# Splitting the output projection of the differential attention over heads, with part of it done amid the attention

## The chip, the cores and the metric

The kernel runs on one core of a Trainium2 chip. Its time is the device time of one execution in microseconds (us); the median of several executions is compared. The engines are TensorE (PE in the profile, its weight loads as PEld), VectorE (DVE), ScalarE (ACT), GpSimd (POOL) and SyncE (SP), which only issues transfers here. Each engine runs its instructions in the order in which they were laid out when the program was built.

## What is computed

One inference step of a decoder of two layers: layer 0 mixes tokens by gated linear attention, layer 1 by differential attention, and each is followed by an MLP with squared ReLU. There is a prompt of 1024 tokens (16 meta tokens ahead of it) and eight running sequences with one new token each, which read a paged cache. The part that matters here is the prompt in layer 1:

```python
def diff_core(q, k, v, q_pos, k_pos, lam):
    s = jnp.einsum('bqhmd,bkhmd->bhmqk', q, k).astype(F32) * (DIFF_DH ** -0.5)
    ...
    p = jax.nn.softmax(s, axis=-1)
    a = p[:, :, 0] - lam * p[:, :, 1]
    return jnp.einsum('bhqk,bkhe->bqhe', a, v.astype(F32))

def diff_output(o, g_sub, lam_init, w_out, dtype):
    B, T = o.shape[:2]
    o = rms_norm(o, g_sub) * (1.0 - lam_init)
    return o.reshape(B, T, DIFF_HEADS * DIFF_DV).astype(dtype) @ w_out

def post_norm(x, f, g, b):
    return layer_norm(DEEPNORM_ALPHA * x + f, g, b)
```

There are 8 heads; each has two score maps (m = 0, 1) of 64 dimensions and values of 128. The outputs of the heads stand side by side in 1024 columns, so the 1024 rows of w_out belong to the heads, 128 rows each, and the product with w_out is a sum over heads. It is added to the residual and normalised.

## The kernel before

Everything is in fp32 accuracy. Where a product has to keep it, each operand is split into a high part (rounded to fp32r) and the remainder, and three matmuls are made for one: high*high, high*low, low*high (`mm3`, L185 to L188). Weights come in pieces of 128x512 by DMA into `raw` (2 buffers); ACT rounds a piece into `whi` (L173) and POOL subtracts to give `wlo` (L174). A unit of 256 columns is a `whi`/`wlo` pair of 2048 columns, of which there are two.

A tile framework allocates buffers from rotating pools and puts each engine's instructions in order when the program is built, by a timeline of its own. So an instruction can stand before or behind where the source has it. PSUM has three pools: `mmt` (3 buffers), `axt` (3) and `smt` (2).

Attention of layer 1 (L1225 to L1251) goes over heads 0 to 7 and in each over eight blocks of 128 queries, called tiles, in the order 7, 1, 5, 3, 6, 0, 4, 2 (head 7: 3, 2, 1, 0, 7, 6, 5, 4); tile t sees 16 + 128(t + 1) keys. With the first tile of a head, `prep` makes the keys and queries of the next: loads on SP, transposes on TensorE (L1134, L1139, L1144), the split by ACT and VectorE (L182, L183), and nine moves by DMA from POOL's queue (L1150 to L1156). A tile (`tile_`, L1159 to L1202) then does:

- scores on TensorE into `mmt` (L1178, L1179; head 0: L1174 to L1176), in up to three pieces for each of the two maps;
- mask and running minimum on VectorE (L1182) into a score buffer `as` of pool `scp` (5 buffers, 8.3 KB in each partition);
- exponent with row sum on ACT (L1184), and the combination of the two maps on VectorE (L1186 to L1188);
- transposes on TensorE into `axt` (L1197), a copy on ACT into `aT` (L1199, pool `a3`, 6 buffers), and the product with the values on TensorE into `smt` (L1202).

After each four tiles the result goes to `Y` (L1237) with its sum of squares (L1238, L1239). `o_norm` (L1206 to L1214) scales pairs of heads: after heads 1, 3 and 5 two heads at a time, after head 6 that one, with the power and the multiply on POOL; head 7's two halves are multiplied on VectorE. `o_fm` (L1216 to L1222) transposes one head's output of 512 tokens (`c` = 0 or 1) into `XH` and `XL` (high and low), by four transposes (L1220), one ACT copy and one VectorE operation. All eight heads' `o_fm` for c = 0 stand behind tile 3 of head 7, all for c = 1 behind the last tile. `Y` serves for the outputs of the heads until then; afterwards the residual, which was put aside in DRAM (`xres`), is loaded back into the same memory (L1261, eight DMAs).

Then `w_out` (L882 to L908) multiplies: four units of 256 columns (u) by two halves of the tokens (c), in the order written at L886, with two PSUM tiles of 48 matmuls each (2 blocks of tokens, 8 heads, 3 matmuls), 768 in all, and adds each tile to the residual in `Y` (L900). Weights of a unit are loaded when first named. After its fifth tile stands the w_out of the eight running sequences (`samples`, L1300 to L1313). `normalize` (L918) takes the finished rows, `to_fm` (L944) transposes them for the MLP, whose weights and buffers (`hp`, `HF`, `rwp`) get their memory when the attention's pools close.

Of the kernel before, what the change touches and what calls it, by code (L numbers as in the profile page):

```python
# [11 lines left out]
F32 = mybir.dt.float32  # L12
F32R = mybir.dt.float32r
# [3 lines left out]
ALU = mybir.AluOpType  # L17
# [12 lines left out]
FF = 4096  # L30
NPG = 32
ALPHA = 4.0 ** 0.25
EPS = 1e-5
# [77 lines left out]
def hybrid_step(ctx, tc, A, dbg=None, upto=9):  # L111
# [769 lines left out]

    def w_out(w, scaled, side=None):  # L882

        units = {}
        n = 0
        for u, c in ((0, 0), (1, 0), (0, 1), (1, 1), (2, 0), (3, 0), (2, 1), (3, 1)):  # L886
# [3 lines left out]
            for i2 in range(2):  # L890
                ps = mmt()
                t0 = 4 * c + 2 * i2
                for i in range(2):
                    a = slice((t0 + i) * P, (t0 + i + 1) * P)
                    for k in range(NB):
                        mm3(ps[:, i * 256 : (i + 1) * 256], XH[:, k, a], XL[:, k, a], hv[:, k, :], lv[:, k, :], k == 0, k == NB - 1)
                yv = Yt[:, t0 : t0 + 2, u * 256 : (u + 1) * 256]
                pv = ps.rearrange("p (i n) -> p i n", n=256)
                if scaled:
                    V.tensor_tensor(yv, yv, pv, op=ALU.add)  # L900
                else:
                    steps_v.append(V.scalar_tensor_tensor(yv, yv, ALPHA, pv, ALU.mult, ALU.add).ins)
                if side and (n == 4 if scaled else n < 5):
# [127 lines left out]
    paged = decode()  # L1031
    normalize(w_out(A["gla_w_out"][0], False, paged), stats, lambda c: to_fm(c, 0))
    normalize(mlp(paged), stats, lambda c: to_fm(c, 1))
# [181 lines left out]

    def o_fm(h, c):  # L1216
        cs = slice(512 * c, 512 * c + 512)
        ps = axt()
        for i in range(4):
            TE.transpose(ps[:, i * P : (i + 1) * P], Yt[:, 4 * c + i, h * P : (h + 1) * P], ident)  # L1220
        S.activation(XH[:, h, cs], ps, AF.Copy, scale=gs)
        V.scalar_tensor_tensor(XL[:, h, cs], ps, gs, XH[:, h, cs].bitcast(F32), ALU.mult, ALU.subtract)  # L1222
# [29 lines left out]

# [5 lines left out]
    rwp = e.enter_context(tc.tile_pool(name="rwp", bufs=5))  # L1258
    for c in range(2):
        for u in range(4):  # L1260
            dma(Yt[:, 4 * c : 4 * c + 4, u * 256 : (u + 1) * 256], A["xres"][512 * c : 512 * c + 512, u * 256 : (u + 1) * 256].rearrange("(t p) n -> p t n", p=P))  # L1261
    CH = TH // 2

    HF = hp.tile([P, NB, 2, TH], F32, name="HF")

# [306 lines left out]
```

## Time and profile before

| | |
|---|---|
| runs | 2924.56, 2924.34, 2919.79 us; median 2924.34 us |
| span of the profiled execution, first to last instruction | 2919.7 us |
| busy share of the span | PE 95%, DVE 65%, ACT 36%, POOL 39% |
| mean granted TensorE clock | 0.976 |
| attention of layer 1 | about 1814 to 2089 us of the span |
| its w_out, with the normalisation and the transposes amid it | about 2089 to 2194 us |
| DMA over the whole span | 636 MB, 218 GB/s |

The profiled execution's own time isn't listed apart from its span; the span is 0.1 us under the lowest run. In the views, a group of instructions stands as line, engine, operation, output<-inputs, shape and count, then busy us in total, mean ns of one, and the idle time before them with what ended it. In a window's row come busy us (and count) of PE, PEld, DVE, ACT and POOL, then the granted clock (1.00 is full), the busy share of the DMA engines and GB/s. A wait reads "engine, tile and line <- what it waited for: us in total, times, longest". The ends of matmuls are modelled, so a busy TensorE needn't be at its peak rate.

### The profile page before, as it was taken

The numbers are of one execution on the slowest core, as the hardware profiler recorded it, in microseconds if no ns is written. First come the engines' busy times: TensorE is split into PE (matmuls) and PEld (weight loads), VectorE is DVE, ScalarE is ACT, GpSimd is POOL, SyncE is SP. The second block draws the span as 40 slices with busy tenths as digits, with TensorE's granted clock in tenths as the row PEclk, the third lists the DMA queues.
The fourth block names the chain that finished last, engine by engine and source line by source line (L and its number), as shares of the span: only waits on it lengthen the run. The fifth ranks groups of instructions, "written<-read, shape, count | busy, mean of one in ns | idle before, by whom it ended". The sixth has DMA issues, their size and how long they took to land. (4 is left out here: it accounts for less than half of the span.)

```text
span 2919.7 us, 52085 instructions
## 1 busy us (share of the span) xinstructions
PE 2779.7 (95%) x19653; PEld 2277.6 (78%) x19653; DVE 1891.2 (65%) x2982; ACT 1044.1 (36%) x2075; POOL 1133.7 (39%) x867
## 2 busy tenths in 40 slices
PE   8889999999999999999999998889998999999997
PEld 5666767987777777777898896778888889797885
DVE  2564644457877777777667942788638855838478
ACT  3233453251222122122321112667524535335352
POOL 2230222233333334334233331132335766677664
PEclk9899999999999999999999998999999999999998
DMA  7557651514798988988387999363436778595893
GB/s 257 178 185 251 233 177 37 198 56 141 242 350 297 335 309 298 346 317 321 137 275 252 348 343 314 75 139 86 119 112 205 195 207 232 152 281 129 257 246 87
DMA packets 285366, 636.46 MB, mean 218 GB/s; under 512 B 25510, under 2 KB 141292, under 8 KB 273852
## 3 DMA queue, kind: packets, MB, share of 16 engines
q1 hardware_dynamic: 252716, 520.66, 51.6%
q0 software_dynamic: 32400, 112.50, 15.9%
q8 instruction: 154, 2.52, 0.4%
q14 instruction: 96, 0.79, 0.1%
HBM read 575.55 MB, written 44.06 MB: 212 GB/s over the span
## 5 line engine op out<-in xcount | busy, mean ns | idle before, releaser
L174 POOL TENSOR_TENSOR wlo<-raw,whi 128x512 fp32r<-128x512 f32 x256 | 360.0, 1419 | 744.0 <-ACT whi L173 670.8
L186 PE MATMUL mmt<-whi,XH 128*128 128x256 f32 (+1 forms) x1760 | 527.4, 302 | 2.9 <-ACT Y L310 2.0
L187 PE MATMUL mmt<-wlo,XH 128*128 128x256 f32 (+1 forms) x1760 | 527.8, 301 | 0.7 <-POOL wlo L174 0.7
L186 PE MATMUL mmt<-XH,whi 128*128 128x512 f32 (+1 forms) x1216 | 438.1, 361 | 7.4 <-DVE HL L183 7.2
L188 PE MATMUL mmt<-whi,XL 128*128 128x256 f32 x1536 | 437.2, 286 | 0.1
L188 PE MATMUL mmt<-XH,wlo 128*128 128x512 f32 (+1 forms) x1216 | 434.4, 358 | 0.0
L790 DVE TENSOR_REDUCE sc<-pg 128x16 f32<-128x1024 f32 x256 | 309.7, 1214 | 93.4 <-POOL pg L789 90.1
L173 ACT CAST whi<-raw 128x512 fp32r<-128x512 f32 x256 | 152.9, 619 | 578.4 <-PE mmt L188 191.1
L186 PEld LDWEIGHTS mmt<-whi,XH 128*128 128x128 f32 x1760 | 333.4, 190 | 30.1 <-issue 15.6
L187 PEld LDWEIGHTS mmt<-wlo,XH 128*128 128x128 f32 x1760 | 334.8, 190 | 28.2 <-issue 16.8
L187 PE MATMUL mmt<-XL,whi 128*128 128x512 f32 x768 | 307.3, 400 | 0.0
L188 PEld LDWEIGHTS mmt<-whi,XL 128*128 128x128 f32 x1536 | 292.1, 191 | 9.9 <-issue 8.8
L789 DVE TENSOR_TENSOR pg<-pg,qb 128x1024 f32<-128x1024 f32 x192 | 256.8, 1343 | 62.1 <-DMA pg<-in_cache_k 38.1
L186 PEld LDWEIGHTS mmt<-XH,whi 128*128 128x128 f32 x1216 | 231.7, 191 | 55.1 <-issue 13.7
L789 POOL TENSOR_TENSOR pg<-pg,qb 128x1024 f32<-128x1024 f32 x64 | 158.6, 2478 | 293.5 <-DMA pg<-in_cache_k 236.7
L188 PEld LDWEIGHTS mmt<-XH,wlo 128*128 128x128 f32 x1216 | 231.8, 191 | 35.8 <-issue 3.8
L186 PE MATMUL mmt<-whi,HH 128*128 128x512 f32 x512 | 205.6, 402 | 1.7 <-DVE Y L1014 1.7
L187 PE MATMUL mmt<-wlo,HH 128*128 128x512 f32 x512 | 204.7, 400 | 0.0
L188 PE MATMUL mmt<-whi,HL 128*128 128x512 f32 x512 | 203.9, 398 | 0.0
L187 PEld LDWEIGHTS mmt<-XL,whi 128*128 128x128 f32 x768 | 145.4, 189 | 39.6 <-issue 8.8
L1416 POOL TENSOR_TENSOR wlo<-RW,whi 128x512 fp32r<-128x512 f32 x96 | 156.3, 1749 | 37.1 <-ACT whi L1415 37.0
L1416 POOL TENSOR_TENSOR wlo<-rw,whi 128x512 fp32r<-128x512 f32 x92 | 147.7, 1674 | 41.4 <-ACT whi L1415 41.2
(441 smaller groups left out, 5769.3 us busy)
## 6 DMA issues: line engine op xcount, KB each, us to landing
pg<-in_cache_k SPq DMA_DIRECT2D x256, 512.0 KB, 6.0
pg<-in_cache_v SPq DMA_DIRECT2D x256, 512.0 KB, 6.0
XH<-xc POOLq DMA_DIRECT2D x42, 1032.0 KB, 7.9
raw<-in_mlp_w SPq DMA_DIRECT2D x164, 256.0 KB, 3.5
swt<-in_mlp_w SPq DMA_DIRECT2D x32, 1024.0 KB, 5.6
rw<-in_mlp_w SPq DMA_DIRECT2D x116, 256.0 KB, 3.8
RW<-in_mlp_w POOLq DMA_DIRECT2D x96, 256.0 KB, 6.0
xc<-XH POOLq DMA_DIRECT2D x14, 1032.0 KB, 6.8
```

Source lines behind the costliest of these rows:

```text
L173: S.copy(hi[:, c], raw)
L174: G.tensor_tensor(lo[:, c], raw, hi[:, c].bitcast(F32), op=ALU.subtract)
L186: TE.matmul(ps, ah, bh, start=first, stop=False)
L187: TE.matmul(ps, ah, bl, start=False, stop=False)
L188: TE.matmul(ps, al, bh, start=False, stop=last)
L789: eng.tensor_tensor(pg, pg, qb, op=ALU.mult)
L790: return V.tensor_reduce(sc[:, n, :], pg.rearrange("p (h d) -> p h d", d=64), op=ALU.add, axis=AX.X).ins
L1416: G.tensor_tensor(lo[:, k, :], t, hi[:, k, :].bitcast(F32), op=ALU.subtract)
```

## The change

The rows of w_out are split between heads 0 to 2 (`EH = 3`) and heads 3 to 7.

*Early part.* A generator, `early_out`, is stepped from the loop over heads. Its first six steps (head 2, tiles 0 to 3; head 3, n = 0 and 2) run `o_fm` for heads 0 to 2 into new buffers `OH` and `OL` (12 KB each in a partition). The other sixteen steps each make one PSUM tile of 18 matmuls (2 blocks of tokens, 3 heads, 3 matmuls) for one u and one pair of token blocks: at head 3, n = 4 and 6; heads 4, 5 and 6, n = 0, 2, 4 and 6; head 7, n = 0 and 1. ACT copies the tile to an `aT` buffer, and a DMA from POOL's queue adds it to `xres` in DRAM (256 KB each). The weights of the three heads for one u (768 columns) lie in the free end of the two `XL` buffers and are loaded, rounded and subtracted anew after each four tiles (`halves_of`).

*Room.* The pool of score buffers has 4 instead of 5. `o_norm` on POOL comes after head 1 (heads 0 and 1), head 2 (that head), head 4 (heads 3 and 4) and head 6 (heads 5 and 6).

*Late part.* `o_fm` of heads 3 to 7 writes to places 0 to 4 of `XH` and `XL`. The residual is loaded back in two halves, each behind the `o_fm` of its half. `late_out` goes over the two halves of the tokens outside and the four units inside, keeps all four units' weights (two in `whi`/`wlo`, two in `WF`, which shares its memory with `HF`), and makes 16 PSUM tiles of 30 matmuls, 480 in all. `samples` follows the third of them instead of the fifth.

```diff
-    def w_out(w, scaled, side=None):
+    def w_out(w, side):
...
-    scp = e.enter_context(tc.tile_pool(name="scp", bufs=5))
+    scp = e.enter_context(tc.tile_pool(name="scp", bufs=4))
...
-    def o_fm(h, c):
+    def o_fm(h, c, hi=None, lo=None):
         cs = slice(512 * c, 512 * c + 512)
+        if hi is None:
+            hi, lo = XH[:, h - EH, cs], XL[:, h - EH, cs]
...
+    def reload(c):
+        for u in range(4):
+            dma(Yt[:, 4 * c : 4 * c + 4, u * 256 : (u + 1) * 256], A["xres"][512 * c : 512 * c + 512, u * 256 : (u + 1) * 256].rearrange("(t p) n -> p t n", p=P))
+
+    OH = a1.tile([P, EH, T], F32R, name="OH")
+    OL = a1.tile([P, EH, T], F32R, name="OL")
+    wo = A["diff_w_out"][0].rearrange("(k p) n -> p k n", p=P)
+    wv_ = [x.rearrange("p a n -> p (a n)")[:, 3088 : 3088 + 256 * EH] for x in XL.t]
+
+    def halves_of(hi, lo, k0, u):
+        for x in range(0, hi.shape[1], 512):
+            w = min(512, hi.shape[1] - x)
+            raw = wrp.tile([P, 512], F32, name="raw")
+            dma(raw[:, :w].rearrange("p (k n) -> p k n", n=256), wo[:, k0 + x // 256 : k0 + (x + w) // 256, u * 256 : (u + 1) * 256])
+            S.copy(hi[:, x : x + w], raw[:, :w])
+            G.tensor_tensor(lo[:, x : x + w], raw[:, :w], hi[:, x : x + w].bitcast(F32), op=ALU.subtract)
+
+    def out_tile(xh, xl, w, nk, t0):
+        hv, lv = (x.rearrange("p (k n) -> p k n", n=256) for x in w)
+        ps = mmt()
+        for i in range(2):
+            a = slice((t0 + i) * P, (t0 + i + 1) * P)
+            for k in range(nk):
+                mm3(ps[:, i * 256 : (i + 1) * 256], xh[:, k, a], xl[:, k, a], hv[:, k, :], lv[:, k, :], k == 0, k == nk - 1)
+        return ps
+
+    def early_out():
+        halves_of(*wv_, 0, 0)
+        for h in range(EH):
+            for c in range(2):
+                cs = slice(512 * c, 512 * c + 512)
+                o_fm(h, c, OH[:, h, cs], OL[:, h, cs])
+                yield
+        for u in range(4):
+            for t0 in range(0, 8, 2):
+                ps = out_tile(OH, OL, wv_, EH, t0)
+                o = a3.tile([P, 4, P], F32, name="aT").rearrange("p j q -> p (j q)")
+                S.copy(o, ps)
+                nc.gpsimd.dma_start(A["xres"][t0 * P : (t0 + 2) * P, u * 256 : (u + 1) * 256].rearrange("(i p) n -> p i n", p=P), o.rearrange("p (i n) -> p i n", n=256), accum_op=ALU.add)
+                if t0 == 6 and u < 3:
+                    halves_of(*wv_, 0, u + 1)
+                yield
...
             if n == 3 and h == 7:
                 o_norm(V, slice(0, 4), slice(7, 8))
-                for j in range(8):
+                for j in range(EH, 8):
                     o_fm(j, 0)
-        if h < 6 and h % 2:
-            o_norm(G, slice(0, 8), slice(h - 1, h + 1))
-        elif h == 6:
-            o_norm(G, slice(0, 8), slice(6, 7))
+                reload(0)
+            if h == 2 and n < 4 or h == 3 and n in (0, 2, 4, 6) or 3 < h < 7 and n % 2 == 0 or h == 7 and n < 2:
+                next(early)
+        if h in (1, 2, 4, 6):
+            o_norm(G, slice(0, 8), slice(2 if h == 2 else h - 1, h + 1))
     o_norm(V, slice(4, 8), slice(7, 8))
-    for j in range(8):
+    for j in range(EH, 8):
         o_fm(j, 1)
+    reload(1)
     e.close()
...
+    def late_out():
+        side, n, us = samples(), 0, []
+        for c in range(2):
+            for u in range(4):
+                if c == 0:
+                    if u < 2:
+                        w = [wsp.tile([P, 2048], F32R, name=x)[:, :LW] for x in ("whi", "wlo")]
+                    else:
+                        w = [WF[:, x : x + LW] for x in (2 * LW * (u - 2), 2 * LW * (u - 2) + LW)]
+                    halves_of(*w, EH, u)
+                    us.append(w)
+                for t0 in (4 * c, 4 * c + 2):
+                    ps = out_tile(XH, XL, us[u], NB - EH, t0)
+                    yv = Yt[:, t0 : t0 + 2, u * 256 : (u + 1) * 256]
+                    V.tensor_tensor(yv, yv, ps.rearrange("p (i n) -> p i n", n=256), op=ALU.add)
+                    if n == 2:
+                        next(side)
...
-    normalize(w_out(A["diff_w_out"][0], True, samples()), stats, lambda c: to_fm(c, 2, xr))
+    normalize(late_out(), stats, lambda c: to_fm(c, 2, xr))
+    HF = hp.tile([P, NB, 2, TH], F32, name="HF", tag="HF")
```

More of the change, by code (lines that the diff above doesn't have):

```diff
@@ L31 @@
 NPG = 32
+EH = 3
 ALPHA = 4.0 ** 0.25
@@ L1031, in hybrid_step @@
     paged = decode()
-    normalize(w_out(A["gla_w_out"][0], False, paged), stats, lambda c: to_fm(c, 0))
+    normalize(w_out(A["gla_w_out"][0], paged), stats, lambda c: to_fm(c, 0))
     normalize(mlp(paged), stats, lambda c: to_fm(c, 1))
@@ L1225, in hybrid_step @@
+    early = early_out()
     nxt = prep(0)
@@ L1258, in hybrid_step @@
     rwp = e.enter_context(tc.tile_pool(name="rwp", bufs=5))
-    for c in range(2):
-        for u in range(4):
-            dma(Yt[:, 4 * c : 4 * c + 4, u * 256 : (u + 1) * 256], A["xres"][512 * c : 512 * c + 512, u * 256 : (u + 1) * 256].rearrange("(t p) n -> p t n", p=P))
     CH = TH // 2
-    HF = hp.tile([P, NB, 2, TH], F32, name="HF")
+    LW = 256 * (NB - EH)
+    WF = hp.tile([P, NB, 2, TH], F32R, name="WF", tag="HF").rearrange("p a c n -> p (a c n)")
     RX = hp.tile([P, 4 * TH], F32, name="RX")
```

15 lines of the change are left out of this document (8 added, 7 removed).

## The prediction

> **What bounds the kernel now.** I read the page first (span, engine shares, clock), then windows over the attention and over w_out of layer 1, then the waits of the attention.
>
> ```profile
> span 2919.7 us, 52085 instructions
> PE 2779.7 (95%) x19653; PEld 2277.6 (78%) x19653; DVE 1891.2 (65%) x2982; ACT 1044.1 (36%) x2075; POOL 1133.7 (39%) x867
> PE 21%; DVE 6%; DMA 5%; issue 3%; POOL 2%; ACT 1%; DVEq 0%; POOLq 0%; ACTq 0%
> ```
>
> TensorE is busy for 95% of the span, so a matmul is only cheaper elsewhere if TensorE idles there. Windows (columns: busy us of PE, PEld, DVE, ACT, POOL with counts, then granted clock, DMA share, GB/s): heads 3 to 7 as a whole, then head by head in their first and second halves, then w_out, and a dense stretch of matmuls of 128x256.
>
> ```profile
> 1917.00:2089.00 172.00, 156.18 (x1129) 142.02 (x1128) 144.32 (x450) 121.73 (x285) 41.45 (x47) 0.96 0.43 99
> 1917.00:1930.00 13.00, 10.78 (x59) 8.18 (x58) 12.56 (x44) 9.55 (x22) 3.06 (x6) 0.93 0.57 135
> 1930.00:1951.00 21.00, 21.00 (x169) 20.82 (x168) 17.43 (x61) 15.73 (x37) 1.53 (x3) 0.96 0.63 108
> 1951.00:1963.00 12.00, 10.54 (x67) 7.98 (x66) 11.46 (x38) 10.20 (x25) 4.37 (x4) 1.00 0.57 152
> 1963.00:1984.00 21.00, 17.42 (x134) 16.77 (x133) 17.09 (x45) 12.38 (x31) 6.78 (x8) 0.92 0.49 103
> 1984.00:1997.00 13.00, 11.06 (x64) 9.13 (x63) 12.22 (x43) 9.67 (x25) 3.56 (x7) 0.87 0.43 99
> 1997.00:2016.00 19.00, 19.00 (x155) 18.71 (x154) 15.85 (x60) 15.29 (x39) 1.02 (x2) 1.00 0.40 88
> 2049.00:2089.00 40.00, 37.19 (x287) 33.90 (x288) 28.81 (x81) 25.93 (x57) 9.99 (x7) 1.00 0.25 80
> 2089.00:2194.00 105.00, 103.84 (x787) 91.17 (x786) 39.83 (x81) 25.62 (x39) 38.92 (x27) 1.00 0.46 143
> 2160.00:2181.00 21.00, 21.00 (x181) 21.00 (x180) 12.25 (x35) 7.61 (x9) 1.39 (x2) 1.00 0.08 27
> 2222.00:2240.00 18.00, 16.01 (x121) 15.79 (x121) 16.79 (x14) 12.01 (x27) 15.23 (x15) 0.91 0.75 197
> 2240.00:2257.00 17.00, 8.35 (x66) 7.93 (x65) 16.89 (x10) 3.37 (x6) 10.92 (x11) 0.86 0.82 236
> ```
>
> A head takes about 33 us and has two halves. In the first 12 or 13 us VectorE is full (12.56 of 13, 11.46 of 12, 12.22 of 13) and TensorE issues one matmul per 0.2 us; here masks and minima set the pace. In the rest TensorE is full in two of three heads (21.00 of 21, 19.00 of 19) and VectorE has 3 to 4 us to spare; here transposes and A*V set it. Over heads 3 to 7 TensorE idles 172 - 156.18 = 15.8 us. w_out behind it is TensorE alone: 103.84 of 105. The waits of eight heads (us in total, times, longest) say the same from both sides:
>
> ```profile
> DVE as L1182 <- PE mmt L1179: 23.9, 22, 4.5
> PEld mmt L1178 <- DVE ast L1182: 11.6, 25, 1.3
> PE axt L1197 <- DVE as L1188: 7.1, 5, 3.5
> ```
>
> VectorE waits for score matmuls twice as long as these wait for VectorE to free PSUM, so extra matmuls ahead of scores also hurt VectorE.
>
> **The change part by part.** One matmul of 128x256 costs, start to start, 21.00/181 = 0.116 us (the 2160 window).
>
> *Late w_out.* The rows of w_out that ran after the attention:
>
> ```profile
> L187 PE MATMUL mmt<-wlo,XH 128*128 128x256 f32 x230 | 65.2, 285 | 0.0
> L186 PE MATMUL mmt<-whi,XH 128*128 128x256 f32 x229 | 64.9, 287 | 0.5 <-ACT whi L173 0.5
> L188 PE MATMUL mmt<-whi,XL 128*128 128x256 f32 x229 | 64.7, 284 | 0.0
> L174 POOL TENSOR_TENSOR wlo<-raw,whi 128x512 fp32r<-128x512 f32 x12 | 15.3, 1281 | 38.9 <-ACT whi L173 38.9
> ```
>
> That is 688 of 768. The changed kernel has 480 (5 heads of 8), and its order puts 56 of them ahead of the last A*V, so 424 follow: 264 fewer, 264 x 0.116 = 30.6 us off the path. Against it, hand-over: the order of SyncE puts the third raw piece of unit 1 behind the reloads of the residual, which wait for the last o_fm, and units 2 and 3 convert into a region that is free only after the attention. Before, whole units were ready (idle 0.5 us). Two chunks (one load and one ACT and POOL conversion, 1.28 us each on POOL) can be late: 0 to +6 us, taken +3, as unit 0 (two tiles of 30 matmuls, 7 us) covers part.
>
> *Early blocks.* 16 blocks of 18 matmuls are added inside heads 3 to 7: 288 x 0.116 = 33.4 us of TensorE. Ends: 0, if all falls where VectorE sets the pace; +33.4, if all falls where TensorE does. The order of the changed kernel puts the blocks behind bursts of score matmuls, about half of them in either half of a head, and the idle TensorE is 15.8 us. Taking that as filled: 33.4 - 15.8 = +17.6. Each block also has one ACT copy and an accumulating DMA of 256 KB issued by POOL; their nearest rows:
>
> ```profile
> L1199 ACT COPY aT<-axt 128x512 f32<-128x512 f32 x64 | 36.8, 581 | 24.7 <-PE axt L1197 24.4
> RW<-in_mlp_w POOLq DMA_DIRECT2D x96, 256.0 KB, 6.0
> ```
>
> The copy is 0.58 us ( ACT has 50 us idle in these 172). The DMA, 6.0 us to landing, is one of 16 in 140 us at a DMA share of 0.43, and the reload that reads them comes some 30 us after the last (head 7's second tile against the end of the attention): cost nothing. If POOL is late, the copy's aT buffer (one of six) comes back late and the copies for A*V wait; that is the third rival.
>
> *Weights of heads 0 to 2.* Four sets, each of a 512 and a 256 column piece, on ACT and POOL. Three come amid heads 4 to 6. POOL works 41 of 172 us there, so its own time is free. But:
>
> ```profile
> 1899.28 4.73 DVE L1188 SCALAR_TENSOR_TENSOR as<-as,ast 128x528 f32<-128x528 f32 x1
> 1899.78 3.65 POOL L1214 TENSOR_TENSOR Y<-Y,orr 128x2048 f32<-128x2048 f32 x1
> L174 POOL TENSOR_TENSOR wlo<-raw,whi 128x512 fp32r<-128x512 f32 x8 | 10.5, 1326 | 37.9 <-ACT whi L173 37.9
> ```
>
> The combine L1188 of this width took 4.73 us and ended when POOL's multiply did. If each subtract holds up VectorE once, three sets cost 3 x (1.33 + 0.7) = 6 us; ends 0 and +6, taken +1, since VectorE is combining for under a fifth of the time and a 1.3 us overlap is a third of the one shown. The Trainium skill, "SBUF — State Buffer", section "SBUF: two separate sides", calls the port pair of VectorE and GpSimd an exclusive lock held for the whole instruction, when VectorE reads two SBUF inputs against a GpSimd operation that reads SBUF; the two rows agree (4.73 us beside 3.65). By that rule alone every subtract that meets a combine blocks it, and the sum would come out 5 us higher than mine.
>
> *Score buffers, five to four.* A fifth tile's mask must now wait until the transposes of the tile four before it have read their buffer. In head 4, tile 7's last transposes and the first mask of the fourth tile after it (464 wide):
>
> ```profile
> 1961.19 0.27 PE L1197 MATMUL axt<-c_ident,as 128*128 128x128 f32 x1
> 1959.98 0.63 DVE L1182 CUSTOM_DVE_ANT_0 as<-mmt,cmask 128x464 f32<-128x464 f32 x1
> ```
>
> The mask began 1.5 us before the transposes ended; it would now wait, in the half that VectorE bounds, and the masks and combines behind it on VectorE with it. That is the worst kind of tile (tile 7, once per head): 0 to 8 x 1.5 = 12 us; taken +3, as the queue behind it has slack in the second half.
>
> *o_fm of heads 0 to 2* moves from head 7 and after it into heads 2 and 3: six times four transposes, one ACT copy, one VectorE operation.
>
> ```profile
> L1221 ACT ACTIVATE XH<-axt,gs 128x512 fp32r<-128x512 f32 x15 | 10.1, 687 | 5.0 <-PE axt L1220 4.9
> L1222 DVE SCALAR_TENSOR_TENSOR XL<-axt,gs,XH 128x512 fp32r<-128x512 f32 x13 | 9.7, 748 | 7.0 <-ACT XH L1221 6.9
> ```
>
>  On VectorE 6 x 0.75 = 4.5 us are added where it is nearly full, and as much is taken from the end: 0 to +4, taken +1. The o_norm pieces stay four multiplies on POOL.
>
> *Start of the attention.* The mask table's buffer lies elsewhere, and its fill and load now wait for the last of decode.
>
> ```profile
> 1802.22 0.33 DVE L1102 MEMSET cmask<- 128x320 f32 x1 [11.56 <-SPq L756]
> 1813.76 0.23 DVE L846 COPY oT<-smt 128x4 f32<-128x4 f32 x2 [7.82 <-PE smt L844]
> 1814.31 0.53 DVE L1182 CUSTOM_DVE_ANT_0 as<-mmt,cmask 128x352 f32<-128x352 f32 x1 [0.32 <-DVE oT L846]
> raw<-in_mlp_w SPq DMA_DIRECT2D x164, 256.0 KB, 3.5
> ```
>
> Before, the fill was 11 us ahead of the first mask. Now it stands directly ahead: at least the 0.33, at most that and a load (3.5 us for one four times as large); taken +2.
>
> *Behind w_out.* With tokens outer, the first 512 tokens are done with half of the late work (240 matmuls, 28 us) still to come, against a quarter (192, 22 us) before. VectorE gets them 6 us earlier, and in 2222 to 2257 it is full (16.79 of 18, 16.89 of 17) while TensorE idles 2.0 + 8.6 us: -5 to +3 (the weights of the MLP have 28 us less to arrive), taken -2.
>
> *Clock.* Heads 3 to 7 ran at 0.96 of the clock, 0.04 x 172 = 6.9 us lost. Denser matmuls may keep it up; 0 to -7, taken -2, since 1930:1951 lost clock with TensorE full. The Trainium skill, "TensorE: Matmul & The Clock Gate", section "What's actually happening", has the clock fall to half after an idle window of about 3.4 us and rise after as much sustained work. By that rule blocks in the idle stretches would give all of it back, and the sum would be 5 us lower; the trace agrees only in part, as 1951:1963 idled 1.5 us and kept 1.00.
>
> Sum: -30.6 + 3 + 17.6 + 1 + 3 + 1 + 2 - 2 - 2 = **-7.0 us**. It stands against the profiled span of 2919.7; the median of the runs, 2924.3, is 4.6 above that (what lies around the span isn't shown; the lowest run is 2919.8). The difference goes on the median: **2917.3 us**.
>
> **The rivals.**
>
> *Slower: the blocks don't fit into the idle time.* A block of 18 is 2.1 us in one piece, and TensorE's gaps in the first half are shorter (1.5 to 2.2 us in all of it). A block ahead of the next scores then delays VectorE there, and in the second half it delays transposes. For it: VectorE already waits 23.9 us for score matmuls. Against it: one matmul per 0.2 us in the first halves. Price: all 33.4 us instead of 17.6, so +15.8 - 7.0 = +8.8, 2933. It decides against the change from 24.6 us exposed (74%) on.
>
> *Larger gain.* TensorE in the first halves waits on VectorE, so half of the blocks (16.7 us) cost nothing, and those of the second half meet the remaining idle time (21 - 17.42 = 3.6 us in one head) and the lost clock: exposed some 10 instead of 17.6, clock -7 instead of -2: -7.0 - 7.6 - 5 = -19.6, 2905. Against it: nothing is idle in the two full second halves.
>
> *POOL late.* The accumulating DMA and the moves of the next head share POOL's queue; a move behind a subtract that waits for its load holds up the next head's scores. If each of heads 4 to 6 starts 5 us late, 15 us: +8, 2932. Against it, a move of head 2 for head 3:
>
> ```profile
> 1903.65 0.56 POOL L1156 DMA_DIRECT2D XH<-XH  x1 [0.22 <-issue]
> ```
>
> It is issued 13 us before head 3 begins (1917). That the change merely moves work at no net effect is the sum with 24 us exposed, about 2924.
>
> **How the numbers follow.** Forecast 0.45 (its own range 2911 to 2925, between 10 and 25 us exposed); slower by unfit blocks 0.31; larger gain 0.13; POOL late 0.11. A measurement of this kernel tells about 0.2% (5.8 us) from no change. Of the forecast 0.29 lies below -5.8, the rest within. Faster 0.29 + 0.13 = 0.42; same 0.16 + 0.03 of the slower cases = 0.19; slower 0.39. The range reaches from the larger gain with a bit of its own spread (2901) to the slower cases with the buffer and port costs at their upper ends (2933 + 7): 2901 to 2940.
>
> **What would show it.** Late w_out: 424 matmuls between the last A*V and normalize, about 50 us with under 6 us idle. Early blocks: heads 3 to 7 take some 189 instead of 172 us, minus or plus the small terms, with the idle TensorE near zero; if they take over 200, the slower rival holds; under 183, the larger gain. Buffers: VectorE's masks waiting for the transposes once per head. Port: a combine stretched beside a subtract of a 512 piece. Start: the first mask later than 0.6 us after the last copy of decode. Clock: 0.96 or more in these heads. The prediction is wrong if the time lies in the attention's other heads, or if late w_out idles over 10 us for weights.

## The result, and the profile after

The changed kernel is slower: 2947.1 us median (2945.4 to 2950.4) against 2922.1 us, a ratio of 1.0089 with a 95% interval of 1.0073 to 1.0105. The forecast was 2917.3 us, faster, with a range up to 2940. The page of the changed kernel:

```profile
span 2947.8 us, 52159 instructions
PE 2777.4 (94%) x19653; PEld 2268.5 (77%) x19653; DVE 1884.7 (64%) x2982; ACT 1055.7 (36%) x2095; POOL 1145.8 (39%) x887
```

TensorE has as many instructions and as much busy time as before (2779.7 us); the 28.1 us by which the two spans differ are idle time. To see where, both executions are cut at three events: the last copy of decode (L846 before, L847 after), the last A*V, and the last transpose for the MLP. Two windows of the kernel before (attention; late stage):

```profile
1814.00:2088.70 274.70, 247.47 (x1739) 223.41 (x1740) 223.75 (x707) 187.34 (x442) 58.28 (x69) 0.94 0.45 99
2088.70:2211.90 123.20, 120.53 (x922) 106.95 (x920) 51.47 (x100) 37.11 (x55) 49.02 (x37) 1.00 0.49 152
```

and of the changed kernel:

```profile
1822.40:2131.70 309.30, 278.84 (x2023) 253.62 (x2024) 222.97 (x712) 202.61 (x467) 82.81 (x92) 0.95 0.50 103
2131.70:2238.70 107.00, 92.83 (x638) 76.83 (x636) 50.94 (x97) 32.42 (x48) 43.08 (x34) 0.92 0.56 169
```

| stage | before, us | after, us | difference | forecast |
|---|---|---|---|---|
| start of the span to the last copy of decode | 1814.0 | 1822.4 | +8.4 | 0 (start of the attention +2) |
| attention, to the last A*V | 274.7 | 309.3 | +34.6 | +20.6 beside the start (17.6 + 1 + 3 + 1 - 2) |
| late stage, to the last transpose for the MLP | 123.2 | 107.0 | -16.2 | -27.6 (-30.6 + 3) |
| MLP, to the end | 707.8 | 709.1 | +1.3 | -2 |

TensorE idled 274.7 - 247.47 = 27.2 us in the attention before and 309.3 - 278.84 = 30.5 us after: 33.4 us of matmuls went in and none of the idle time was filled. In the late stage it idled 2.7 us before and 14.2 us after.

The same two attentions, cut once more at the last A*V of head 2: heads 0 to 2 and heads 3 to 7 before, then after.

```profile
1814.00:1918.60 104.60, 93.00 (x625) 82.90 (x626) 80.74 (x262) 66.26 (x159) 16.84 (x22) 0.90 0.48 96
1918.60:2088.70 170.10, 154.48 (x1116) 140.51 (x1115) 143.01 (x446) 121.08 (x284) 41.45 (x47) 0.96 0.44 101
1822.40:1928.00 105.60, 93.17 (x650) 83.37 (x651) 82.64 (x283) 72.28 (x169) 17.06 (x24) 0.92 0.39 82
1928.00:2131.70 203.70, 185.66 (x1374) 170.25 (x1374) 140.33 (x430) 130.34 (x299) 65.75 (x68) 0.97 0.56 115
```

Heads 0 to 2, where no block stands, took 1.0 us more. Heads 3 to 7, which hold all sixteen blocks, took 33.6 us more, with 15.6 us of idle TensorE before and 18.0 us after.

VectorE's waits in the changed attention (beside those quoted in the prediction):

```profile
DVE as L1180 <- PE mmt L1177: 37.1, 37, 4.9
PEld mmt L1176 <- DVE ast L1180: 13.0, 26, 2.0
PE axt L1195 <- DVE as L1186: 4.6, 3, 3.1
```

VectorE now waits 37.1 us for score matmuls, 23.9 before. And TensorE at the end of decode, before and after, a row each, with the idle time ahead in brackets:

```profile
1810.14 1.18 PE L830 MATMUL smt<-pg,sc 128*16 128x256 f32 x16 [0.85 <-DMA pg<-in_cache_v]
```

```profile
1807.01 1.05 PE L831 MATMUL smt<-pg,sc 128*16 128x256 f32 x8 [10.44 <-DMA pg<-in_cache_v]
1810.72 1.05 PE L831 MATMUL smt<-pg,sc 128*16 128x256 f32 x8 [2.66 <-DMA pg<-in_cache_v]
1814.39 1.05 PE L831 MATMUL smt<-pg,sc 128*16 128x256 f32 x8 [2.61 <-DMA pg<-in_cache_v]
```

The last pages of the cache arrive late in the changed kernel, though no edit is in decode.

### The profile page after: what moved, and what is told of

Its sections match the earlier page's. It is cut to its first block, busy times and chain, and to the rows that moved or that the text cites. A ratio compares the mean times of both kernels' runs of the same rounds, so it can differ in the third digit from the quotient of the medians.

```text
span 2947.8 us, 52159 instructions
## 1 busy us (share of the span) xinstructions
PE 2777.4 (94%) x19653; PEld 2268.5 (77%) x19653; DVE 1884.7 (64%) x2982; ACT 1055.7 (36%) x2095; POOL 1145.8 (39%) x887
## 5 line engine op out<-in xcount | busy, mean ns | idle before, releaser
L175 POOL TENSOR_TENSOR wlo<-raw,whi 128x512 fp32r<-128x512 f32 x240 | 336.8, 1416 | 691.1 <-ACT whi L174 616.8
L187 PE MATMUL mmt<-whi,XH 128*128 128x256 f32 (+1 forms) x1584 | 477.5, 303 | 6.1 <-ACT whi L1240 3.6
L188 PE MATMUL mmt<-wlo,XH 128*128 128x256 f32 (+1 forms) x1584 | 477.5, 302 | 1.6 <-POOL wlo L1241 0.8
L189 PE MATMUL mmt<-whi,XL 128*128 128x256 f32 x1360 | 387.8, 286 | 0.0
L174 ACT CAST whi<-raw 128x512 fp32r<-128x512 f32 x240 | 143.4, 619 | 536.7 <-PE mmt L189 191.9
L187 PEld LDWEIGHTS mmt<-whi,XH 128*128 128x128 f32 x1584 | 300.6, 191 | 30.3 <-issue 12.7
L188 PEld LDWEIGHTS mmt<-wlo,XH 128*128 128x128 f32 x1584 | 301.6, 191 | 25.8 <-issue 13.5
L189 PEld LDWEIGHTS mmt<-whi,XL 128*128 128x128 f32 x1360 | 259.1, 191 | 5.8 <-issue 5.1
L189 PE MATMUL mmt<-whi,HL 128*128 128x512 f32 x512 | 203.7, 398 | 0.0
```

Of the source, the lines that this page charges most:

```text
L174: S.copy(hi[:, c], raw)
L175: G.tensor_tensor(lo[:, c], raw, hi[:, c].bitcast(F32), op=ALU.subtract)
L187: TE.matmul(ps, ah, bh, start=first, stop=False)
L188: TE.matmul(ps, ah, bl, start=False, stop=False)
L189: TE.matmul(ps, al, bh, start=False, stop=last)
```

## The experiments

Each experiment's stages are measured as above. Seven executions whose attention was not meant to differ (the changed kernel, no_accum, held_moves, samples_later, late_order, samples_ready, all_mended) have attentions of 305.6 to 313.6 us, mean 309.7; differences of 4 us between single profiles are not read. Heads 3 to 7 alone, cut at the last A*V of head 2, take 198.4 to 203.7 us in these seven, mean 201.2.

### What the blocks cost: no_blocks and thin_blocks

```diff
 for t0 in range(0, 8, 2):
-    ps = out_tile(OH, OL, wv_, EH, t0)
-    o = a3.tile([P, 4, P], F32, name="aT").rearrange("p j q -> p (j q)")
-    S.copy(o, ps)
-    nc.gpsimd.dma_start(A["xres"][t0 * P : (t0 + 2) * P, u * 256 : (u + 1) * 256].rearrange("(i p) n -> p i n", p=P), o.rearrange("p (i n) -> p i n", n=256), accum_op=ALU.add)
...
```

> The changed kernel without its 16 early blocks (their matmuls, copies and accumulating DMAs); everything else stays, so rows of heads 0 to 2 are missing from the product. The attention, from the last copy of decode to the last A*V, took 274.7 us before and 309.3 us after. If the 33.4 us of matmuls are exposed in full and nothing else costs (theory), it falls to about 276 us, and the whole is about 33 us below the changed kernel. If smaller terms (four score buffers, o_fm amid heads 2 and 3, subtracts beside combines) carry a good part (rival), it stays at 285 to 295 us. If the blocks cost even more than their matmuls, it falls below 274 us.

```diff
             for k in range(nk):
+                if thin:
+                    TE.matmul(ps[:, i * 256 : (i + 1) * 256], xh[:, k, a], hv[:, k, :], start=k == 0, stop=k == nk - 1)
+                    continue
                 mm3(ps[:, i * 256 : (i + 1) * 256], xh[:, k, a], xl[:, k, a], hv[:, k, :], lv[:, k, :], k == 0, k == nk - 1)
...
```

(`thin` holds in the early blocks only)

> The changed kernel with 6 matmuls instead of 18 in each early block: the products with the low parts are left out there, so the output is less exact. Runs of the changed order so far have an attention of 306 to 314 us, without blocks 280.9. Theory (the cost is TensorE's time, 28 us for 33.4 us of matmuls): a third of it stays, attention 288 to 293 us. Rival (the cost is the block as such: a PSUM buffer taken from the scores, a place ahead of scores): 300 us or more.

The attention of no_blocks, then of thin_blocks:

```profile
1819.70:2100.60 280.90, 248.98 (x1733) 226.20 (x1734) 223.16 (x712) 191.02 (x448) 61.87 (x75) 0.92 0.44 98
```

```profile
1826.30:2120.20 293.90, 258.31 (x1832) 234.24 (x1833) 225.53 (x712) 200.25 (x466) 82.88 (x92) 0.94 0.53 109
```

Over the whole attention, blocks of 18 matmuls cost 309.3 - 280.9 = 28.4 us for 33.4 us of matmuls, and blocks of 6 cost 13.0 us for 11.1. But these differences hold something beside the blocks: heads 0 to 2, where none stands, took 113.6 us in no_blocks and 105.6 in the changed kernel. Heads 3 to 7 alone, cut at the last A*V of head 2, in no_blocks and in thin_blocks:

```profile
1933.30:2100.60 167.30, 149.34 (x1084) 137.44 (x1084) 135.61 (x432) 118.24 (x279) 40.35 (x46) 0.96 0.44 100
1934.60:2120.20 185.60, 162.35 (x1183) 148.20 (x1183) 142.94 (x431) 127.89 (x298) 65.90 (x68) 0.96 0.61 126
```

They took 167.3 us without blocks (166.4 to 171.9 in the four other traces that have none) and 198.4 to 203.7 with full ones: 31 to 36 us more than in no_blocks, so about all of the 33.4. Thin blocks cost 18.3 us there for 11.1 us of matmuls. So full blocks cost about their time on TensorE, as the theory had it. What one matmul more costs, and what a block costs as such, can't be told from one execution each; that thin_blocks' attention came out 1 us above its range (288 to 293) is within the scatter. TensorE's idle time in heads 3 to 7 is 18.0 us without blocks, 23.3 with thin and 18.0 with full ones: nothing of it is filled, whatever is put beside it. The whole of no_blocks took 2915.2 us, 0.9991 of before (0.9981 to 1.0002): with the blocks' work left out altogether, the rest of the change only breaks even. That of thin_blocks took 2933.3 us (1.0043, 1.0027 to 1.0058).

### Whether place, size or PSUM pool matters: blocks_front, blocks_back, half_blocks, axt_blocks

```diff
-            if h == 2 and n < 4 or h == 3 and n in (0, 2, 4, 6) or 3 < h < 7 and n % 2 == 0 or h == 7 and n < 2:
+            if h == 2 and n < 4 or h == 3 and n in (0, 2, 4, 6) or 3 < h < 7 and n < 4 or h == 7 and n < 2:
```

(blocks_front; blocks_back has n > 3 in the same place)

> The changed kernel with the blocks of heads 4 to 6 behind tiles 0, 1, 2 and 3 of the head's order instead of 0, 2, 4 and 6, so nearer to the half that VectorE paces. My prediction: absorbed there, exposed in the other half: attention 295 to 302 us. Theory B (place is of no matter): 306 to 312 us. If blocks hurt VectorE's half more (they stand ahead of scores): 312 us or more.

> The changed kernel with the blocks of heads 4 to 6 behind the last four tiles of each head. With all of them behind the first four (blocks_front) the attention took 318.1 us. If blocks hurt most where VectorE sets the pace, as that run suggests against my prediction: 298 to 305 us. If crowding four blocks in a row hurts wherever it is: 314 us or more. If place is of no matter: 306 to 313 us.

```diff
-                ps = out_tile(OH, OL, wv_, EH, t0)
...
+                for i in range(2):
...
+                    ps = mmt()
...
+                    for k in range(EH):
+                        mm3(ps[:, :256], OH[:, k, a], OL[:, k, a], hv[:, k, :], lv[:, k, :], k == 0, k == EH - 1)
...
+                    S.copy(o[:, 256 * i : 256 * i + 256], ps[:, :256])
+                    if i == 0:
+                        yield
...
```

(half_blocks: a step of the generator for each half)

> The changed kernel with 32 early blocks of 9 matmuls (one block of tokens each) instead of 16 of 18, one behind each tile of heads 4 to 6. The 16 blocks cost the attention 28.3 us of their 33.4 (309.2 against 280.9 without them). Theory A (a block in one piece of 2.1 us starves VectorE of score tiles, finer ones fit into the gaps): attention 297 to 302 us. Theory B (TensorE is what limits every part of a head once the moves and weight loads between matmuls are counted, so there is nothing to fill): 307 to 312 us.

```diff
-                ps = out_tile(OH, OL, wv_, EH, t0)
+                ps = out_tile(OH, OL, wv_, EH, t0, axt)
...
```

> The changed kernel with the early blocks in the PSUM pool of the transposes (three buffers) instead of that of the scores (three). Theory (TensorE's time): 305 to 314 us as before. Rival (a block takes one of three score buffers for 2.7 us and VectorE runs dry; its waits for scores rose from 23.9 to 37.1 us): VectorE's waits fall back to 25 us and the attention to 295 to 303 us, unless the transposes now wait as long.

The attentions of blocks_front, blocks_back, half_blocks and axt_blocks, in this order:

```profile
1827.90:2146.00 318.10, 284.84 (x2023) 258.12 (x2024) 224.87 (x711) 202.38 (x466) 82.79 (x92) 0.93 0.48 100
```

```profile
1828.60:2139.40 310.80, 277.82 (x2003) 255.87 (x2004) 217.75 (x711) 201.09 (x466) 82.37 (x92) 0.93 0.51 104
```

```profile
1817.70:2136.10 318.40, 280.12 (x2016) 254.63 (x2017) 228.65 (x713) 203.51 (x482) 83.73 (x92) 0.95 0.49 100
```

```profile
1824.10:2130.40 306.30, 277.69 (x2017) 257.40 (x2018) 219.73 (x711) 201.10 (x465) 83.48 (x92) 0.93 0.51 105
```

None is better than the changed kernel's 309.7 by more than the scatter. The wholes, as ratios to the kernel before and in the same order, are 1.0136, 1.0104, 1.0129 and 1.0083, against 1.0089. The framework chose the places, so they differ less than the edits do: of the 288 matmuls, 100 stand in the first 13 us of a head (counted from the last A*V of the head before) in blocks_front, 54 in the changed kernel and 18 in blocks_back. With more of them in the half that VectorE paces, where my prediction had them absorbed, the attention took 8 us more; with more in the other half it took as long as mixed. Finer blocks cost 9 us more, above the ranges of both theories: VectorE's waits for scores rose to 53.2 us there. A PSUM pool of their own doesn't help (VectorE's waits stay at 39.2 us), so it wasn't the score buffers that VectorE missed. What is left is TensorE's time itself. That is by exclusion: no run put blocks at the very places where TensorE waits, so a better place isn't ruled out.

### Whether POOL is late: no_accum

```diff
                 S.copy(o, ps)
-                nc.gpsimd.dma_start(A["xres"][t0 * P : (t0 + 2) * P, u * 256 : (u + 1) * 256].rearrange("(i p) n -> p i n", p=P), o.rearrange("p (i n) -> p i n", n=256), accum_op=ALU.add)
```

> The changed kernel without the 16 accumulating DMAs; blocks are multiplied and copied, and not added, so rows of heads 0 to 2 are missing from the sum. Theory (TensorE's time is exposed): attention unchanged at 309 us within 3 us. Rival (POOL is late with the DMA and aT buffers come back late): attention falls by 5 to 15 us.

Its attention:

```profile
1823.30:2135.70 312.40, 282.15 (x2023) 257.08 (x2024) 222.02 (x711) 202.76 (x466) 62.68 (x76) 0.94 0.41 89
```

312.4 us, 2953.4 us in all (ratio 1.0114, 1.0096 to 1.0132): the 16 accumulating DMAs cost nothing that shows. The other half of my third rival, moves held up behind subtracts, doesn't show either: TensorE's scores waited 4.4 us for moves in the changed attention and 4.7 us before, and no_blocks, which keeps the subtracts, has heads 3 to 7 at 167.3 us. So that rival falls.

### Buffers and grouping: before_four, before_norms, no_blocks_ofm_late

```diff
-    scp = e.enter_context(tc.tile_pool(name="scp", bufs=5))
+    scp = e.enter_context(tc.tile_pool(name="scp", bufs=4))
```

(in the kernel before)

> The kernel before with four score buffers instead of five, nothing else. My prediction took +3 us of 0 to 12. Theory: attention 275 to 280 us. If the buffers are a main cause of the longer attention (rival): 285 us or more. If they cost nothing: 274 to 276 us.

```diff
-        if h < 6 and h % 2:
-            o_norm(G, slice(0, 8), slice(h - 1, h + 1))
-        elif h == 6:
-            o_norm(G, slice(0, 8), slice(6, 7))
+        if h in (1, 2, 4, 6):
+            o_norm(G, slice(0, 8), slice(2 if h == 2 else h - 1, h + 1))
```

(in the kernel before)

> The kernel before with o_norm on POOL after heads 1, 2, 4 and 6 (the changed kernel's grouping) instead of 1, 3, 5 and 6, nothing else. If the grouping makes the attention longer by 6 us: 279 to 282 us. If not: 273 to 276 us, and the 6 us stay unexplained.

```diff
-            if h == 2 and n < 4 or h == 3 and n in (0, 2, 4, 6) or 3 < h < 7 and n % 2 == 0 or h == 7 and n < 2:
-                next(early)
+            if h == 7 and n == 3:
+                for _ in range(6):
+                    next(early)
```

(in no_blocks; the generator is stepped no further, so the three later sets of weights, with their subtracts, are left out too)

> The kernel without blocks (no_blocks, rows of heads 0 to 2 are missing), with the six o_fm of heads 0 to 2 and the loads of their weights in head 7 instead of heads 2 to 6. no_blocks had an attention of 280.9 us against 274.7 before. If the moved o_fm and weights cause the difference: 273 to 277 us. If it is scatter between executions or comes from four score buffers with the other grouping of o_norm: 279 us or more.

The attentions, in this order:

```profile
1817.30:2091.80 274.50, 245.78 (x1739) 221.07 (x1740) 218.01 (x707) 187.37 (x442) 60.09 (x69) 0.95 0.44 99
```

```profile
1815.60:2083.50 267.90, 243.30 (x1742) 218.94 (x1743) 215.18 (x708) 186.13 (x441) 57.92 (x69) 0.96 0.47 102
```

```profile
1818.30:2098.40 280.10, 246.88 (x1739) 224.73 (x1740) 213.09 (x712) 188.38 (x444) 58.33 (x70) 0.93 0.42 94
```

The fifth buffer is worth nothing in the attention (274.5 against 274.7; whole 1.0011, 0.9997 to 1.0026). The other grouping of o_norm doesn't lengthen it: 267.9 us, shorter if anything, though the whole is not told from before (0.9990, 0.9973 to 1.0008). The moved o_fm and the subtracts aren't it either (280.1 against 280.9; whole 0.9999, 0.9981 to 1.0018). So some 6 us of the changed attention, between 274.7 and 280.5, stay without a cause. They lie in heads 0 to 2, ahead of the blocks: 101.5 to 104.6 us in the three traces of the kernel before's form, 105.4 to 113.6 in the fifteen of the changed one, while heads 3 to 7 without blocks take as long as before. What was not tried alone: the later fill of the mask table, and the order that the framework makes of all this together.

### The end of decode: held_moves

```diff
-        move = nc.gpsimd.dma_start
+        def move(o, i):
+            with tc.issue_after(vz):
+                nc.gpsimd.dma_start(o, i)
```

(`vz` is the last fill of the value buffers on POOL)

> The changed kernel with POOL's moves for head 1 put behind the fill of the value buffers (which waits for the last of decode), as they stood before the change. In the trace the last copy of decode came at 1822.4 us against 1814.0, with TensorE waiting 17 us for the last cache pages, while the moves had been issued at 1794 instead of 1805. Theory (the moves' traffic holds up the last pages): decode ends at 1814 to 1816 us and the whole is about 7 us shorter than the changed kernel. Rival (the later end is variation between executions, or comes of other transfers): decode ends at 1820 to 1823 as in the changed kernel.

POOL's first moves for head 1 before the change, with the fill ahead of them, and after it, from the timelines:

```profile
1802.23 0.34 POOL L1110 MEMSET vm<- 128x128 f32 x2 [47.44 <-SPq L756]
1804.68 0.75 POOL L1150 DMA_DIRECT2D XH<-XH  x1 [1.22 <-ACT XH L182]
1805.42 0.54 POOL L1152 DMA_DIRECT2D XH<-XL  x1
```

```profile
1794.08 0.75 POOL L1148 DMA_DIRECT2D XH<-XH  x1 [1.62 <-ACT XH L183]
1795.02 0.53 POOL L1150 DMA_DIRECT2D XH<-XL  x1 [0.19 <-issue]
```

Before, two fills waited for decode's memory until 1802.2. POOL's, of the value buffers, stood first in POOL's queue. VectorE's, of the mask table (the row with 11.56 us of waiting in the prediction), stood ahead of VectorE's part of head 1's split, so that the first move waited another 1.22 us for ACT's part. Together they held the moves until the last page had been issued (1804.0). In the changed kernel both fills come later in their queues (the buffers' memory lies elsewhere), and six moves of 256 KB start ahead of the last pages. held_moves brings back POOL's hold alone. In it decode ended at 1817.6 us, between the two expectations, and the whole took 2938.7 us (ratio 1.0062, 1.0045 to 1.0080, against 1.0089); its profiled execution was the slowest of four, and the two intervals overlap, so the whole alone doesn't decide. The end point scatters by some us: 1805.6 to 1817.6 in the six traces whose moves come late (mean 1814.1), 1817.0 to 1828.6 in the twelve others (mean 1822.8). The time from the issue of the last page to the last copy separates them: 10.0, 10.0 and 9.3 us in the three traces with the kernel before's order there (before, before_four, before_norms), 10.7 to 11.2 in the three with held moves (held_moves, all_mended, two_heads), and 17.2 to 22.4 in the other twelve. The theory holds: the moves cost the last pages 7 to 11 us. The queues in the changed kernel's last 28 us of decode:

```profile
q1 hardware_dynamic: 5000, 5.10, 74.9%
q0 software_dynamic: 560, 1.85, 30.1%
```

POOL's queue (q0) takes 30% of the 16 engines' time for 1.85 MB. The Trainium skill, "DMA: Bandwidth & Descriptors", section "Queues, rings and completion order", says that each DMA engine takes turns between the queues that have work, packet by packet. The trace agrees as far as it shows: both queues moved data in this stretch (5.10 and 1.85 MB), and the last page, once issued, took 21.7 us to the last copy.

### The late stage: samples_later, late_order, samples_ready, all_mended

TensorE's waits in the changed kernel's late stage, and POOL's power ahead of the third, from the timelines:

```profile
2134.20 0.39 PE L188 MATMUL mmt<-wlo,XH 128*128 128x256 f32 x1 [0.85 <-POOL wlo L1241]
2140.71 0.80 PE L187 MATMUL mmt<-whi,XH 128*128 128x256 f32 x2 [3.63 <-ACT whi L1240]
2156.55 3.59 PE L507 MATMUL smt<-rw,zoT 128*32 128x512 f32 x10 [6.46 <-DVE zoT L1357]
2164.93 1.05 PE L507 MATMUL smt<-rw,zoT 128*32 128x512 f32 x2 [2.23 <-DMA rw<-in_diff_w_out]
```

```profile
2143.02 10.55 POOL L1353 TENSOR_TENSOR zoq<-zoq,mhalf 128x64 f32<-128x64 f32 x1
```

```diff
-                    if n == 2:
+                    if n == 4:
                         next(side)
...
-        for c in range(2):
-            for u in range(4):
+        for c, u in ((0, 0), (1, 0), (0, 1), (0, 2), (0, 3), (1, 1), (1, 2), (1, 3)):
```

(samples_later has the first edit, late_order both)

> The changed kernel with the w_out of the eight running sequences behind the fifth tile of the late part, as in the kernel before, instead of the third. Late stage (last A*V to the last transpose for the MLP): 123.3 us before with 2.7 us of idle TensorE, 107.1 us after with 14.2 idle, of which 6.5 wait for the power of POOL and the two multiplies of VectorE ahead of that product. Theory: with two more tiles (60 matmuls, 7 us) ahead these 6.5 us go: late stage 100 to 102 us, whole about 6 us less. Rival (the wait moves to the rows of weights or to the last tiles): late stage within 2 us of 107.

> As samples_later, and unit 0 is multiplied for both halves of the tokens before unit 1. After, 56 of unit 0's 60 matmuls for the first half ran ahead of the last A*V, so nothing covered unit 1's weights (4.5 us of idle TensorE at 2134 to 2140). Theory: 60 more matmuls cover them: late stage 96 to 98 us. Rival (the second half's residual, reloaded behind the last o_fm, or its o_fm is late instead): 100 us or more, with VectorE's add or TensorE waiting there.

samples_later: 106.2 us, the same 6.3 us of waiting: the framework put the product where it had been, so the edit changed nothing in TensorE's order (whole 1.0113, 1.0094 to 1.0133). late_order filled most of that wait (0.85 left), not all of the one for unit 1's weights (2.9 left of 4.5), and the last matmul of w_out came 82.8 us after the last A*V instead of 91.1. But TensorE then idled 3.3 us for rows of weights and 5.7 us for the operands of the MLP's first half, and the stage ended at 106.1 us (whole 1.0076, 1.0058 to 1.0095): the idle time moved on.

```diff
+    def sam_pre():
+        V.tensor_tensor(oq, oT, oT, op=ALU.mult)
...
+        G.tensor_tensor(oq, oq, bc(mhalf, [P, 8, NS], 1), op=ALU.pow)
+        V.tensor_tensor(oT, oq, oT, op=ALU.mult)
...
+            if n == 0 and h == 7:
+                sam_pre()
```

(and the same steps taken out of `samples`)

> The changed kernel with the normalisation of the eight running sequences' attention output (squares, sum, POOL's power of 10.5 us) done in head 7 instead of behind the attention. Late stage 107.1 us with 14.2 of idle TensorE, 6.5 of it waiting for that. Theory: the 6.5 us go, late stage 100 to 102 us. Rival (the product of the running sequences then waits for its rows of weights, whose loads stand behind the reload of the residual): late stage 104 us or more, with waits for these rows grown by 3 us or more.

> The changed kernel with three repairs together: POOL's moves for head 1 held behind the end of decode, unit 0 multiplied for both halves of the tokens before unit 1, and the running sequences' normalisation in head 7. Expected from the single steps: about -7 us at decode and, if the idle time of the late part doesn't just move on, -8 to -10 there: 2930 to 2935 us, still slower than the kernel before, as the blocks' 28 us stay. If the idle time moves on: 2937 to 2942 us.

The late stages of samples_ready and all_mended:

```profile
2125.90:2218.70 92.80, 88.34 (x636) 75.78 (x634) 46.46 (x94) 32.44 (x49) 32.09 (x33) 0.96 0.62 195
```

```profile
2116.20:2207.40 91.20, 87.73 (x637) 74.56 (x634) 47.86 (x94) 32.62 (x49) 32.22 (x33) 0.98 0.64 199
```

samples_ready: 92.8 us, 14.2 less, where the theory had 5 to 7 (whole 2931.9 us, 1.0043, 1.0024 to 1.0062). 9.7 us of it are idle time (4.5 left), and 4.5 us are busy time: the wait had also cost the clock. Its rows in the changed kernel (mean of one, then the idle time), and in samples_ready:

```profile
L507 PE MATMUL smt<-rw,zoT 128*32 128x512 f32 x32 | 16.0, 775 | 9.2 <-DVE zoT L1357 6.5 <-DMA rw<-in_diff_w_out 2.7
```

```profile
L507 PE MATMUL smt<-rw,zoT 128*32 128x512 f32 x32 | 12.4, 604 | 0.0
```

The granted clock was 0.92 in the stage of the changed kernel and 0.96 here. With the change's side effects mended together (all_mended) the whole took 2921.2 us, a ratio of 1.0024 (1.0006 to 1.0043), better than the 2930 to 2935 expected: its decode also ended earlier, at 1805.6 us, some of which is scatter.

### Whether a smaller early part wins: two_heads

```diff
-EH = 3
+EH = 2
...
+            if h == 2 and n < 4 or 2 < h < 7 and n % 2 == 0:
```

(in all_mended, with the kernel before's grouping of o_norm)

> all_mended with EH = 2: 16 blocks of 12 matmuls amid heads 3 to 6, o_norm grouped as before the change, 576 late matmuls. Blocks cost 28 us for 18 matmuls and 13 for 6, so 20.5 for 12; the attention would be 274.7 + 20.5 = 295 us, or 301 if the 6 us of the kernel without blocks stay. Late stage 91.2 + 96 x 0.116 = 102.4 us. Whole against all_mended (attention 310.6): -4 us, or +2. Against the kernel before: -3 us, or +3; so 2915 to 2923 us.

Attention and late stage:

```profile
1814.30:2108.30 294.00, 267.10 (x1931) 245.34 (x1932) 222.38 (x713) 200.09 (x462) 96.64 (x97) 0.94 0.55 114
2108.30:2208.30 100.00, 96.59 (x731) 84.29 (x730) 48.83 (x95) 33.52 (x50) 34.82 (x33) 0.98 0.62 185
```

Both sums come near what was worked out (295 and 102.4), the first partly by luck: heads 0 to 2 took 112.7 us of it, and heads 3 to 7 181.3, so there the fifteen blocks of 12 that stand in them cost 14 us over no_blocks, for 20.9 us of matmuls, in one execution. 2919.4 us against 2922.3, a ratio of 0.9998 (0.9980 to 1.0016): no difference from the kernel before. What is saved behind the attention is paid within it; no run that computes the whole product is told from the kernel before as faster.

## Why the prediction was wrong, step by step

- *Late w_out, -30.6 us.* The count (424 matmuls left) and the price were right: with the product's wait gone (4.5 us of idle time left, for unit 1's weights) the stage is 123.2 - 92.8 = 30.4 us shorter.
- *Hand-over, +3 (0 to +6).* This term failed: it measured 30.6 - 16.2 = 14 us. The prediction considered unit 1's weights only (4.5 us idle, as feared, since 56 of unit 0's 60 matmuls stood ahead of the last A*V and left nothing to cover them). It left out the running sequences' product, which before had 13.4 us of TensorE's time in the same stage without a wait, and hung on a 10.5 us power on POOL that the longer w_out had covered. I had costed it at nothing without naming the work that hid it. It waited 6.5 us for that and 2.7 us for its rows of weights; the clock lost behind the waits made up the rest.
- *Early blocks, +17.6.* This step failed: "Taking that as filled: 33.4 - 15.8". Heads 3 to 7 took 33.6 us more than before (203.7 against 170.1), 31 to 36 us more than without blocks, and TensorE's idle time in them was 15.6 us before and 18.0 after. The halves that VectorE paces did not absorb blocks: blocks_front has more of them there and took longer. The first rival (all 33.4) had the size right, and what decided, 74% exposed, was passed; its mechanism, a block in one piece that doesn't fit, did not show: halves didn't fit better. Its price, 2933 us, is still 14 us short of the measured time, because no rival had the late stage's wait or the end of decode. What fits all the runs is that TensorE's idle time comes from the chain score, mask, exponent, transpose, A*V, and that a block ahead of a link shifts the chain behind it by about its own length. No run shows this link by link.
- *Score buffers, +3 (0 to 12).* 0, by before_four. In the changed kernel masks waited for transposes twice, 2.0 us in all, and not once per head. The late transposes that I quoted cost nothing, because VectorE had other work in its queue ahead of that mask, or made the loss up within the head; the runs don't tell which.
- *o_fm +1, subtracts +1.* Moving the o_fm back, with three sets of subtracts left out, changed 0.8 us. Two combines of 784 columns stood beside subtracts in heads 3 to 7 of the changed kernel (1.03 us is the mean of this width before), 1.1 us too long together, as taken:

```profile
1978.59 1.73 DVE L1186 SCALAR_TENSOR_TENSOR as<-as,ast 128x784 f32<-128x784 f32 x1
2055.88 1.45 DVE L1186 SCALAR_TENSOR_TENSOR as<-as,ast 128x784 f32<-128x784 f32 x1
```

  The pair of rows in the prediction shows a combine held up, but it ended 0.6 us behind POOL's multiply, not with it, and had begun 0.5 us ahead of it. So the rows show that the combine took longer beside the multiply, and not which of the two held the other.
- *Start of the attention, +2.* The mask came 0.9 us after the last copy of decode instead of 0.3: the right way, and 0.5 us instead of 2. But the fills had a part that I didn't cost: they had held back head 1's split and moves. That is most of the +8.4 us ahead of the attention (8.7 us between the means of the traces). I followed what is moved past what in SyncE's queue, and not in POOL's and VectorE's.
- *Behind w_out -2, clock -2.* +1.3 and nothing: heads 3 to 7 ran at 0.97 instead of 0.96, and the late stage lost clock (0.92 from 1.00). The rule that idle windows cost the clock (the Trainium skill, "TensorE: Matmul & The Clock Gate", section "What's actually happening") agrees with the trace there: with 6.46 us of idle time ahead of the product and 2.7 us amid it, its matmuls took 775 ns in the mean, and 604 ns without. By the same rule blocks in the attention should have given the clock back; the traces show 0.01 in heads 3 to 7 (0.96 in no_blocks, 0.97 in the changed kernel).
- *Rivals.* Larger gain: no. POOL late: no (no_accum). The prediction's sign for the slower rival was heads 3 to 7 over 200 us: 203.7.

Against the sum: -7.0 forecast, +28.1 in the spans. Of the 35.1 us between them, the early blocks make +16.0 (33.6 instead of 17.6), the attention's other terms -4.0, the late stage +11.4, the end of decode +8.4 and what follows the late stage +3.3.

## What to carry to other kernels

Idle time of an engine inside a chain of dependent steps is not room: before moving work into it, take the chain's own matmuls as fixed and expect to pay most or all of what is put in (31 to 36 us for 33.4 here), unless a run with the same amount of filler shows otherwise. When work behind a stage is removed, list everything that it was covering, down to single long instructions of slow engines, not only the loads of the part that stays. And when a buffer moves, look at what its first write was holding back in the queue of its engine. Last, to price an addition, compare the part that holds it alone: here the difference of the whole attentions was 28.4 us, and that of the heads with the blocks 36 (203.7 against 167.3).

## What was not expected of the hardware

- The power of 128x64 elements took POOL 10.55 us (128x16: about 3 us), longer than 60 matmuls of w_out (7.0 us).
- Six moves of 256 KB from POOL's queue, issued up to 10 us ahead of decode's last page, delayed its end by 7 to 11 us, while the two queues together took 105% of the 16 engines' time (74.9 and 30.1% in the last 28 us of decode).
- Sixteen accumulating DMAs of 256 KB into DRAM cost no time that can be seen (attention 312.4 us without them, 305.6 to 313.6 with).
